# Six PSUM banks shared out two and four instead of three and three, in a two-layer encoder whose order a planner lays out

## The chip, the cores and the metric

The kernel runs on one core of a Trainium2 chip. The metric is the device time of one execution in microseconds (us), as the median of several runs. A profile of one execution shows when each engine worked: TensorE (PE, with its weight loads as PEld), VectorE (DVE), ScalarE (ACT), GpSimd (POOL), and SyncE (SP), which issues the DMAs.

## What is computed

The input is 512 positions by 1024 channels. Layer 0 is an RMSNorm, an input projection to 7168 channels, a gated convolution of width 3 (mixer A), a spatial gating unit with 128x128 position-mixing matrices (mixer B), an output projection and a residual. Layer 1 is another RMSNorm and projection, an RWKV-7 scan in both directions over 16 heads of 64 channels (mixer C), a 2-D Fourier transform over groups (mixer D), an output projection and a residual; a last RMSNorm follows. What matters here is layer 1, above all the scan:

```python
def wkv7_step(state, inp):
    r, w, k, v, a, b = inp
    sa = jnp.einsum('...ij,...j->...i', state, a)
    state = (state * w[..., None, :] + sa[..., :, None] * b[..., None, :]
             + v[..., :, None] * k[..., None, :])
    y = jnp.einsum('...ij,...j->...i', state, r)
    return state, y
...
def odd_layer(h, w_in, mu, w0, w2, a0, a2, k_k, k_a, r_k, lnx_g, lnx_b, fnet_w, w_out):
    p = jnp.einsum('bsd,de->bse', h, w_in)
    pc, zc, fd, zd = jnp.split(p, ODD_SPLITS, axis=-1)
    yc = rwkv7_bidir_branch(pc, mu, w0, w2, a0, a2, k_k, k_a, r_k, lnx_g, lnx_b) * jax.nn.silu(zc)
    yd = fourier_branch(fd, fnet_w) * jax.nn.silu(zd)
    return jnp.einsum('bse,ed->bsd', jnp.concatenate([yc, yd], axis=-1), w_out)
```

## The kernel before, in words

**Dense blocks.** Activations and weights are each split into a high and a low part, and a product is the sum of three (`mm3`, line 551). A dense block is one 128-channel slice of a projection for all 512 positions: 8 slices of the input times 3, so 24 products that add up in one PSUM bank (`pd_...`; `block0`, line 667, in layer 0, `block`, line 911, in layer 1). Layer 1 has blocks named `wa`, `k`, `r`, `v`, `zc`, `fd` and `zd`. DVE and ACT read a finished block out of PSUM (`evac`, line 946), and its bank is free then.

**The scan.** It is cut into chunks of 64 positions, and the heads into 8 units of two heads and two directions, numbered j = 0 to 7. A unit goes through these steps, and each turns on groups of small products whose results stand in PSUM until DVE and ACT have read them:

- `prep` (line 982): `zw` and `za`, decay and rate from a low-rank product; `half` (line 1059) then makes the operands `at`, `ops` on DVE.
- `sums` (`ss`), and `scores` (line 1095): `sm`, and for each half of the chunks `sa` and `sz`, which become `mt`, `am` and `zz`.
- `inverse` (line 1218): the inverse of a triangular matrix, first on DVE (`iL`, `iA`, `iT`, `iF`), then by the products `iH`, `iTT` and `iTB`, `iG`, `iTJ`; each needs what DVE or ACT made of the one ahead (`iTT` and `iTB` read `iHs`, which DVE makes of `iH`). The result is `dz`.
- `fold` (line 1301): `sp` of `zz` and `dz`, read out as `pt`; then `sg` of `ops`, `pt` and `am`, in four groups to a unit, read out as `gq` by a masked multiply on DVE and a copy on ACT.
- `chain` (line 1371): eight steps over the chunks, one after another. DVE makes `X` of `pa`, and PE makes the next `pa`, and the output `py`, of `X` and `gq`. Its tiles `pa` and `py` have a bank each.
- `bonus` (line 1194, `bo`) and `post` (line 1420, `vy`) finish the unit.

**The banks.** PSUM has eight banks here, in four rings. The ring `d` has three, for the dense blocks and for `zw`, `za` and `bo`. The ring `s` has three, for the other small products: `sm`, `sa`, `sz`, `sp` and `sg` take two each, one per head or direction, and ask for both at once (`both`, line 229); `iTT` and `iTB` take one each, at the same time. The output projections spread their four sums over the banks of several rings, by a tuple of tags (`project`, line 565; `project_o`, line 1542).

**The order.** The program is written as strands, generators that yield operations, and a planner (`Plan`, line 159) emits one operation at a time: it keeps a clock for each engine, and at each step takes the operation that can start first by these clocks, with some leaning to strands of lower rank. The chain has rank 0, scores, inverse and fold rank 1, dense blocks rank 5. A strand that asks a ring for a tile when none is free waits until another strand frees one. So the number of banks in a ring sets when a strand may go on, and with it the order on every engine. On the chip each engine then works its instructions off in that order, and waits by semaphores for operands and for banks.

Of the kernel before, what the change touches and what calls it, by code (L numbers as in the profile page):

```python
# [17 lines left out]
PSUM = bass.MemoryType.PSUM  # L18

P = 128  # L20
S = 512
D = 1024
KB = D // P
NS = S // P
C = 64
# [407 lines left out]
class K:  # L433
# [131 lines left out]
    def project(self, name, n, y, res, pair):  # L565

        for d in range(2):
            ps, tags = [None] * NS, (("d", "d", "d", "py"), ("s", "s", "s", "d"))[d]
            for bs in [(b,) for b in range(n - 3)] + ([(n - 3, n - 2, n - 1)] if d == 1 and pair else [(n - 3,), (n - 2,), (n - 1,)]):
                for b in bs:  # L570
                    yield f"w_{name}{d}_{b}"
                for s in range(NS):
                    if ps[s] is None:
                        ps[s] = yield from self.get(tags[s], f"p{name}{d}_{s}", [P, 512])
                    for b in bs:
                        w = self.w[f"{name}{d}_{b}"][0]
                        for e in range(2):
                            yield f"{y}{2 * b + e}"
                            l = self.out[y, 2 * b + e]
                            yield self.mm3(ps[s], self.part(l, slice(0, P), slice(s * P, (s + 1) * P)), self.part(w, slice(0, P), e),  # L580
                                           b == 0 and e == 0, b == n - 1 and e == 1)
                    if bs[-1] == n - 1:
                        self.plan.strand(2, res(d, s, ps[s], tags[s]))
                for b in bs:
                    self.used(f"{name}{d}_{b}")
# [956 lines left out]
    def project_o(self, d):  # L1542

        yield "bonus7"
        if d:
            for g in range(4):
                yield f"yo{8 + g}"
        else:
            self.gb = yield from self.get("vq", "fin_gb", [P, D])
            yield self.Q.dma_start(self.gb, self.I["fin_g"].to_broadcast([P, D]))  # L1550
        ps, tags = [None] * NS, (("d", "d", "d", "s"), ("pa", "s", "s", "py"))[d]
        def part(b, s):
            w = self.w[f"o{d}_{b}"][0]
            if ps[s] is None:
                if d == 1 and s in (1, 3):
                    yield ("y7_1", "vy7")[s // 2]
                ps[s] = yield from self.get(tags[s], f"po{d}_{s}", [P, 512])
            for e in range(2):
                yield f"yo{2 * b + e}"
                l = self.out["yo", 2 * b + e]  # L1560
                yield self.mm3(ps[s], self.part(l, slice(0, P), slice(s * P, (s + 1) * P)), self.part(w, slice(0, P), e), b == OUTS[0] and e == 0, b == OUTS[-1] and e == 1)


        last = OUTS[-LAST[d]:]
        for b in OUTS[:-LAST[d]]:
            yield f"w_o{d}_{b}"
            for s in range(NS):
                yield from part(b, s)
            self.used(f"o{d}_{b}")
        for b in last:  # L1570
            yield f"w_o{d}_{b}"
        if d:
            yield self.A.activation(self.fss[0][:, 2:3], self.eps["rms"], AF.Sqrt)
        for s in range(NS):
            for b in last:
                yield from part(b, s)
            self.plan.strand(2, self.res(d, s, ps[s], tags[s]))
        for b in last:
            self.used(f"o{d}_{b}")
# [57 lines left out]
    def run(self):  # L1637
        I = self.I
        with ExitStack() as ctx:
            self.cp = self.pool(ctx, "consts")  # L1640
            self.wp = self.pool(ctx, "weights")
            self.tp = tp = self.pool(ctx, "work")
            self.ip = self.pool(ctx, "scan")
            dram = self.pool(ctx, "dram", 1, bass.MemoryType.DRAM)
            dp, sp, yp, cp = (self.pool(ctx, name, n, PSUM) for name, n in (("dense", 3), ("short", 3), ("outs", 1), ("chain", 1)))
            self.h1 = dram.tile([S, D], F32, name="h1_dram")
            self.yd = dram.tile([6, P, S], F32, name="y_dram")
            fz = dram.tile([8, P, S], F32, name="f_dram")
            self.fz = {(kind, g): fz[4 * i + g] for i, kind in enumerate(("fd", "zd")) for g in range(4)}
            plan = self.plan = Plan(self.tc, self.nc)  # L1650
            self.T, self.V, self.A, self.G, self.Q = (plan.engine(e) for e in ("PE", "DVE", "ACT", "Pool", "SP"))
            self.h = tuple(self.cp.tile([P, KB, S], F32R, tag=n, name=n, bufs=1) for n in ("hh", "hl"))
            self.xw, self.units = [None, None], [(e, d) for e in range(2) for d in range(2)]
            self.rings = {}
            for tag, shape, bufs in (("lora", [P, 2, P], 2), ("xw", [P, 2, S], 2), ("k", [P, S], 2), ("r", [P, S], 2), ("w", [P, S], 2), ("a", [P, S], 2),
                                     ("kb", [P, S], 2), ("zg", [P, S], 3), ("bon", [P, S], 2), ("y", [P, S], 2), ("vq", [P, 2, S], 2),
                                     ("E", [P, 2, NCH, C + 1], 1), ("ops", [P, 4 * S], 4), ("at", [P, S], 2), ("q", [P, 1024], 5), ("pt", [P, 1024], 1), ("G", [P, 1024], 5), ("dz", [P, 16, C], 2)):
                self.ring(tag, shape, bufs)
            self.ring("lh", [P, 2, P], 1, dt=F32R)
            self.ring("hi", [P, 2, S], 1, dt=F32R)  # L1660
            for tag, shape in (("T", [P, 16, 16]), ("nr", [P, 2, 16]), ("F", [P, 16, 32]), ("A", [P, 16, 16]), ("A2", [P, 16, 16]), ("Dn", [P, 16, 32]), ("Dt", [P, 16, 32])):
                self.ring(tag, shape, 1, self.ip)
            self.ring("X", [P, 4, 64], 2, self.ip)
            self.ring("wq", [P, KB, P], 5, self.wp)
            self.ring("d", [P, S], 3, dp)
            self.ring("s", [P, 8, C], 3, sp)
            self.ring("py", [P, S], 1, yp)
            self.ring("pa", [P, 4, 64], 1, cp)
            self.blocks = [("wa", 0), ("k", 0)] + list(FIRST)
            self.gates = {}  # L1670
            for j in range(7):
                more = [(b, j + n) for b, n in ORDER if j + n < 8 and (b, j + n) not in self.blocks] + list(EXTRA.get(j, ()))
                self.blocks += more
                units = [(kind, q, k) for kind, q in more for k in range(KB)]
                for i, u in enumerate(units):
                    n = i * NCH // len(units) - SLACK
                    if n >= 0:
                        self.gates[u] = f"X{j}_{n}"
            V, G = self.V, self.G
            self.weights = [(f"pv{q}_{i}", I["w_ev"][q, i], [P, 4, 256]) for q in range(4) for i in range(2)]  # L1680
            at = {"xa": 0, "ba": 8, "ca": 16, "za": 24, "ub": 32, "zb": 48}
            for kinds in (("ub", "zb"), ("xa", "ca", "za", "ba")):
                self.weights += [(f"{b}{j}", I["w_e"][at[b] + j], [P, KB, P]) for m in range(4) for b in kinds for j in (2 * m, 2 * m + 1)]
            self.weights += [(f"e{d}_{b}", I["w_eo"][d, b], [P, 2, 512]) for d in range(2) for b in range(8)]
            at = {"wa": 24, "k": 8, "r": 0, "v": 16, "zc": 25, "fd": 33, "zd": 37}
            self.weights += [(f"{b}{j}", I["w_o"][at[b] + j], [P, KB, P]) for b, j in self.blocks]
            self.weights += [(f"o{d}_{b}", I["w_oo"][d, b], [P, 2, 512]) for d in range(2) for b in OUTS]
            self.w, self.wf, self.out, self.g = {}, {}, {}, [{"j": j} for j in range(8)]
            self.yh0, self.yl0, self.fss, self.h2 = {}, {}, {}, [None] * NS
            self.pool_r, self.pool_k, self.pool_t = FLAGS  # L1690
            for rank, gen in ((0, self.chain()), (1, self.start()), (1, self.build()), (3, self.post()), (4, self.loads()), (4, self.splits()), (4, self.prep()),
                              (5, self.products()), (6, self.params1()), (6, self.unit_states()), (FR, self.fnet()), (6, self.reload())):
                plan.strand(rank, gen, rank == 0, rank == 5)
            plan.run()
# [26 lines left out]
```

## Time and profile before

| what | value |
|---|---|
| runs | 1084.24, 1087.21, 1088.44 us; median 1087.21 |
| the profiled execution | 1090.07 us, of which its span is 1088.3 |
| PE busy | 1024.3 us, 94% of the span |
| DVE busy | 651.3 us, 60% |
| ACT busy | 472.7 us, 43% |
| POOL busy | 124.9 us, 11% |
| mean granted clock of TensorE | 0.983 |

The span is the time from the first to the last instruction of the profiled execution. A share of busy time is a mean over the whole span, and the stages differ: layer 0 takes the first 434 us, the eight units of layer 1 lie between 434 and 1036 us, and the last stretch is the output projection. An engine's idle time counts only where that engine sets the pace.

### The profile page before, as it was taken

The page shows a single profiled execution, that of the slowest core. Times are in us where ns is not written, and L with a number is a line of the kernel's source. Part 1 is how long each engine was busy: PE and PEld are TensorE (multiplying, and loading weights), DVE is VectorE, ACT ScalarE, POOL GpSimd, SP SyncE. Part 2 cuts the span into 40 slices and gives each one's busy share as a digit, 9 for nine tenths or more (in the row PEclk, how much of TensorE's full clock was granted, in tenths as well). Part 3 has the DMA queues.
Part 4 walks back from the last instruction along what each step waited for, and adds up shares of the span by engine and source line. Part 5 has one row for each costly group of instructions (what it writes and reads, how often), then busy time and mean ns, then how long its engine had stood idle before and what let it go on. Part 6 is the DMA issues. An engine that isn't in the chain of part 4 may idle for free. (4 is left out here: it accounts for less than half of the span.)

```text
span 1088.3 us, 27301 instructions
## 1 busy us (share of the span) xinstructions
PE 1024.3 (94%) x12024; PEld 839.3 (77%) x12024; DVE 651.3 (60%) x1225; ACT 472.7 (43%) x795; POOL 124.9 (11%) x155
## 2 busy tenths in 40 slices
PE   7999999999999999998898999989988899999997
PEld 6988888888888888876676778767767677777776
DVE  6464444344343336895795858867793976864453
ACT  7232222222222125753565455744644736453253
POOL 1001210010110010220012101321021201110000
PEclk9999999999999999999998999989998999999999
DMA  8322222322223332332012011110121111154033
GB/s 286 105 73 94 81 94 98 97 97 97 96 96 124 130 116 98 100 105 89 8 46 89 3 42 61 49 52 21 41 71 41 60 39 48 60 172 131 30 107 117
DMA packets 32663, 91.51 MB, mean 84 GB/s; under 512 B 4896, under 2 KB 7712, under 8 KB 32544
## 3 DMA queue, kind: packets, MB, share of 16 engines
q1 hardware_dynamic: 32544, 89.77, 25.1%
q8 instruction: 94, 1.54, 0.6%
q14 instruction: 25, 0.20, 0.1%
HBM read 81.82 MB, written 7.86 MB: 82 GB/s over the span
## 5 line engine op out<-in xcount | busy, mean ns | idle before, releaser
L401 PE MATMUL pe<-w_e,yh 128*128 128x512 f32 x256 | 81.5, 398 | 0.0
L401 PE MATMUL sg<-ops 64*128 64x128 f32 x512 | 66.6, 294 | 7.2 <-ACT am L401 2.1
L401 PEld LDWEIGHTS sg<-ops 64*128 64x128 f32 x512 | 53.9, 196 | 17.1 <-issue 3.9
L401 PE MATMUL sg<-pt,am 64*128 64x128 f32 x512 | 60.5, 283 | 0.0
L401 PEld LDWEIGHTS pe<-w_e,yh 128*128 128x128 f32 x256 | 48.1, 188 | 11.6
L401 ACT COPY gq<-sg 128x256 f32<-128x256 f32 x64 | 23.2, 370 | 71.7 <-DVE gq L401 70.5
L401 PEld LDWEIGHTS sg<-pt,am 64*128 64x128 f32 x512 | 52.3, 195 | 0.0
L401 PE MATMUL pd_zc<-hh,w_zc 128*128 128x512 f32 x128 | 50.5, 437 | 1.3 <-DVE w_zc L401 1.3
L401 PE MATMUL pe<-w_e,yl 128*128 128x512 f32 x128 | 50.3, 393 | 0.0
L401 DVE TENSOR_TENSOR w_e<-wf_e,w_e 128x1024 fp32r<-128x1024 f32 (+1 forms) x19 | 20.0, 1074 | 48.0 <-ACT w_e L401 47.8
L401 PE MATMUL pd_r<-hh,w_r 128*128 128x512 f32 x128 | 45.5, 409 | 2.0 <-DVE w_r L401 2.0
L401 DVE TENSOR_TENSOR gq<-sg,c_masks 128x256 f32<-128x256 f32 x64 | 25.6, 416 | 33.7 <-PE sg L401 33.7
L401 PE MATMUL pd_k<-hh,w_k 128*128 128x512 f32 (+1 forms) x144 | 44.6, 372 | 0.0
L401 PEld LDWEIGHTS pa<-X,gq 128*64 128x64 f32 x448 | 30.8, 139 | 17.1 <-issue 3.9
L401 ACT CAST w_e<-wf_e 128x1024 fp32r<-128x1024 f32 (+1 forms) x19 | 16.9, 913 | 62.4 <-PE pe L401 54.6
L401 PE MATMUL pd_v<-hh,w_v 128*128 128x512 f32 x128 | 43.8, 410 | 0.0
L401 PE MATMUL pa<-X,gq 128*64 128x64 f32 x448 | 38.8, 230 | 4.6 <-DVE X L401 2.0
L401 PE MATMUL pa<-c_cen,vq 128*64 128x128 f32 x256 | 42.6, 288 | 0.0
L401 PE MATMUL pd_ub<-hh,w_ub 128*128 128x512 f32 x128 | 40.5, 393 | 0.0
L401 PE MATMUL pd_zb<-hh,w_zb 128*128 128x512 f32 x128 | 40.4, 392 | 0.0
L401 PE MATMUL pd_xa<-hh,w_xa 128*128 128x512 f32 x128 | 40.4, 392 | 0.0
L401 PE MATMUL pd_ca<-hh,w_ca 128*128 128x512 f32 x128 | 40.4, 392 | 0.0
(362 smaller groups left out, 2831.4 us busy)
## 6 DMA issues: line engine op xcount, KB each, us to landing
wf_e<-in_w_eo SPq DMA_DIRECT2D x16, 512.0 KB
wf_o<-in_w_oo SPq DMA_DIRECT2D x12, 512.0 KB
wf_pv<-in_w_ev SPq DMA_DIRECT2D x8, 512.0 KB
wf_ub<-in_w_e SPq DMA_DIRECT2D x8, 512.0 KB
wf_zb<-in_w_e SPq DMA_DIRECT2D x8, 512.0 KB
wf_xa<-in_w_e SPq DMA_DIRECT2D x8, 512.0 KB
wf_ca<-in_w_e SPq DMA_DIRECT2D x8, 512.0 KB
wf_za<-in_w_e SPq DMA_DIRECT2D x8, 512.0 KB
```

Of the source, the lines that this page charges most:

```text
L401: i = op.call(*op.a, **op.kw)
```

## The change

Ring `d` gets two banks instead of three, and ring `s` four instead of three. Three tuples of tags follow: in each of the output projections one or two of the four sums move from a bank of `d` to one of `s`, or the other way. All planner constants stay, and every product is computed as before.

```diff
@@ project
-            ps, tags = [None] * NS, (("d", "d", "d", "py"), ("s", "s", "s", "d"))[d]
+            ps, tags = [None] * NS, (("d", "s", "s", "py"), ("s", "s", "d", "s"))[d]
...
@@ project_o
-        ps, tags = [None] * NS, (("d", "d", "d", "s"), ("pa", "s", "s", "py"))[d]
+        ps, tags = [None] * NS, (("d", "d", "s", "s"), ("pa", "s", "s", "py"))[d]
...
@@ run
-            dp, sp, yp, cp = (self.pool(ctx, name, n, PSUM) for name, n in (("dense", 3), ("short", 3), ("outs", 1), ("chain", 1)))
+            dp, sp, yp, cp = (self.pool(ctx, name, n, PSUM) for name, n in (("dense", 2), ("short", 4), ("outs", 1), ("chain", 1)))
...
-            self.ring("d", [P, S], 3, dp)
-            self.ring("s", [P, 8, C], 3, sp)
+            self.ring("d", [P, S], 2, dp)
+            self.ring("s", [P, 8, C], 4, sp)
```

Through layer 0 PE's order stays as it was; from the second dense block of layer 1 on it is laid out anew. It has the same 7720 matmuls. In an operation's name the first digit is the unit.

The first place is PE's order between the chains of units 0 and 1. Before, the group `sz1_1` (two banks), `ss2` (one bank) and `iTT1` with `iTB1` (two banks) stand close together:

```order
L401 MATMUL sz1_10_4939<-ops3_3213 64x128
L401 MATMUL sz1_11_4940<-ops2_3210 64x128
L401 MATMUL sz1_11_4940<-ops3_3213 64x128
L401 MATMUL ss2_4964<-sq2_4946,ones_98 32x256 x4
L401 MATMUL pd_v2_5041<-hh_84,w_v2_4970 128x512
L401 MATMUL pd_v2_5041<-hl_85,w_v2_4970 128x512
L401 MATMUL iTT1_5052<-iHs1_4795,iDt1_4764 32x32 x64
L401 MATMUL pd_v2_5041<-hh_84,w_v2_4971 128x512
```

And in the changed kernel, where `sz1_1` has moved into the chain of unit 0, and `ss2` behind `iTB1`:

```order
L401 MATMUL sz1_11_4788<-ops3_3213 64x128
L401 MATMUL py0_4508<-gq0_11_4676,X0_7_4764 64x64 x4
L401 MATMUL za2_0_4773<-xw0_3280,lh2_0_4368 128x512
L401 MATMUL iH1_4821<-iD1_4756,off_103 32x32 x64
L401 MATMUL pd_fd2_4987<-hh_84,w_fd2_4866 128x512
L401 MATMUL pd_v2_5007<-hh_84,w_v2_4908 128x512
L401 MATMUL iTT1_4984<-iHs1_4822,iDt1_4757 32x32 x64
L401 MATMUL iTB1_4985<-iDt1_4757,iHs1_4822 32x32 x32
L401 MATMUL ss2_5023<-sq2_5013,ones_98 32x256
```

Here one row stands for a dense block, and the blocks `k2` and `r2` are left out: between `sz1_1` and `iTT1` there are now most of `k2` and the whole of `r2`, `fd2` and `v2`, where two products of `v2` stood.

The second place is PE's order at the inverse of unit 5. Before, `iTT5` follows `iH5` at once:

```order
L401 MATMUL sa5_11_8509<-ops3_3213,at5_1_8017 64x128
L401 MATMUL iH5_8550<-iD5_8527,off_103 32x32 x64
L401 MATMUL iTT5_8676<-iHs5_8551,iDt5_8528 32x32 x64
L401 MATMUL pd_r6_8562<-hh_84,w_r6_8547 128x512
L401 MATMUL iTB5_8677<-iDt5_8528,iHs5_8551 32x32 x32
```

Now the dense block `r6`, and behind it `v6`, come between:

```order
L401 MATMUL za6_1_8718<-xw1_3325,ll_104 128x512
L401 MATMUL iH5_8632<-iD5_8567,off_103 32x32 x64
L401 MATMUL pd_r6_8797<-hh_84,w_r6_8682 128x512
L401 MATMUL pd_r6_8797<-hl_85,w_r6_8682 128x512
L401 MATMUL pd_r6_8797<-hh_84,w_r6_8683 128x512
```

The third place is the same step of unit 4. Before, dense products follow `iH4`:

```order
L401 MATMUL py3_7434<-gq3_01_7431,X3_3_7517 64x64 x4
L401 MATMUL iH4_7585<-iD4_7541,off_103 32x32 x64
L401 MATMUL pd_zc4_6963<-hh_84,w_zc4_6839 128x512
L401 MATMUL pd_zc4_6963<-hl_85,w_zc4_6839 128x512
L401 MATMUL pd_zc4_6963<-hh_84,w_zc4_6840 128x512
```

Now `iH4`, `iTT4` and `iTB4` stand in a row, and the dense block `r5` follows:

```order
L401 MATMUL za5_0_7711<-xw0_3280,ll_104 128x512
L401 MATMUL pd_k5_7093<-hh_84,w_k5_6856 128x512
L401 MATMUL iH4_7562<-iD4_7529,off_103 32x32 x64
L401 MATMUL iTT4_7801<-iHs4_7563,iDt4_7530 32x32 x64
L401 MATMUL iTB4_7802<-iDt4_7530,iHs4_7563 32x32 x32
L401 MATMUL pd_r5_7876<-hh_84,w_r5_7567 128x512
```

All through layer 1 the chains become more compact: the eight steps of a chain, with their `sp`, `sg`, `sz` and `sa`, now stand with few dense products between them in units 0 to 6, and the dense blocks stand together between the chains.

## Rows read from the trace of the kernel before

**Rows 1.** Busy time by stage: stretch; us, then PE, PEld, DVE, ACT, POOL busy, clock, DMA.

```profile
62.00:324.00 262.00, 262.00 (x1178) 216.22 (x1177) 117.20 (x142) 73.32 (x91) 27.78 (x16) 1.00 0.28 93
434.00:535.00 101.00, 91.94 (x1232) 72.31 (x1230) 76.07 (x134) 55.85 (x91) 14.44 (x23) 0.97 0.25 81
535.00:1036.00 501.00, 460.34 (x8478) 370.40 (x8478) 357.87 (x787) 259.18 (x477) 70.35 (x89) 0.97 0.18 58
```

**Rows 2.** The chain that ended last, at its end: start us, us, what.

```profile
1040.12 41.65 PE po L401 x180
```

**Rows 3.** Who PE waited for, 434 to 972 us: total us, times, longest.

```profile
PE iTT L401 <- DVE iHs L401: 7.5, 3, 3.3
...
PE iTT L401 <- DVE zz L401: 2.4, 1, 2.4
...
PE sm L401 <- ACT gq L401: 1.8, 2, 1.2
...
PE sg L401 <- ACT dz L401: 1.7, 2, 1.2
...
PE sg L401 <- ACT gq L401: 1.1, 2, 0.9
...
PE sz L401 <- ACT dz L401: 0.7, 1, 0.7
PE sa L401 <- ACT gq L401: 0.6, 1, 0.6
...
PE sg L401 <- ACT mt L401: 0.6, 1, 0.6
PE sm L401 <- ACT pt L401: 0.6, 1, 0.6
...
PE sa L401 <- ACT pt L401: 0.5, 1, 0.5
```

**Rows 4.** Timeline at 530 us: start us, us, instruction, count [idle before <-releaser].

```profile
530.21 0.30 PE L401 MATMUL sm<-at,ops 64*32 64x64 f32 x4
...
530.77 0.37 ACT L401 COPY gq<-sg 128x256 f32<-128x256 f32 x1 [2.51 <-DVE gq L401]
...
531.20 1.61 PE L401 MATMUL sm<-at,ops 64*32 64x64 f32 x124 [0.69 <-ACT gq L401]
```

**Rows 5.** Timeline of PE at 580 us.

```profile
580.25 1.93 PE L401 MATMUL iTT<-iHs,iDt 32*32 32x32 f32 x128 [2.38 <-DVE zz L401]
```

**Rows 6.** Busy time in the stretches behind that wait, as in rows 1.

```profile
580.00:590.00 10.00, 9.75 (x219) 7.98 (x221) 3.19 (x8) 4.39 (x8) 1.40 (x2) 0.67 0.29 94
590.00:600.00 10.00, 7.81 (x287) 5.92 (x273) 4.63 (x8) 5.47 (x12) 3.00 (x5) 0.83 0.24 71
```

**Rows 7.** Timeline in layer 0: a dense block read, the next but one begun.

```profile
80.38 0.60 ACT L401 ACTIVATE zb<-pd_zb 128x512 f32<-128x512 f32 x1
...
84.48 0.39 PE L401 MATMUL pd_ub<-hh,w_ub 128*128 128x512 f32 x1
```

**Rows 8.** Readers of ring d by tile: duration ns min/median/max, first and last start.

```profile
L401 DVE SCALAR_TENSOR_TENSOR rq<-pd_r,c_pv,rq x16: 740/744/751, 444.5 to 912.8; 128x511 f32<-128x511 f32 x16
L401 ACT ACTIVATE rq<-pd_r,omu x13: 667/686/692, 443.2 to 910.7; 128x512 f32<-128x512 f32 x13
L401 ACT ACTIVATE w<-zw,w0h x16: 667/687/714, 448.3 to 867.5; 128x512 f32<-128x512 f32 x16
```

**Rows 9.** Timeline of PE at the inverse of unit 5.

```profile
826.15 0.70 PE L401 MATMUL iTT<-iHs,iDt 32*32 32x32 f32 x58 [1.49 <-DVE iHs L401]
```

**Rows 10.** Timeline of PE in the chain of unit 0.

```profile
549.57 0.24 PE L401 MATMUL pa<-X,gq 128*64 128x64 f32 x1 [0.60 <-DVE iA L401]
```

**Rows 11.** Busy time in the chains of units 0, 2 and 4, as in rows 1.

```profile
535.00:561.10 26.10, 24.91 (x367) 20.70 (x368) 24.66 (x67) 11.98 (x25) 5.34 (x7) 1.00 0.09 27
...
665.30:684.50 19.20, 19.20 (x346) 16.58 (x346) 18.40 (x60) 7.64 (x18) 1.31 (x2) 1.00 0.14 47
...
800.40:846.60 46.20, 40.33 (x850) 32.97 (x850) 27.70 (x73) 20.32 (x42) 6.39 (x7) 0.93 0.11 34
```
## The prediction

> **What bounds the kernel now.** I read the busy time by stage first, since a share over the whole span says nothing of one stage. In layer 0 PE is busy for all of its 262 us, at full clock [rows 1]; there a change of banks can only cost. Between 434 and 1036 us PE is busy for 91.94 of 101 us and 460.34 of 501 us, so it stands idle for 9.1 + 40.7 = 49.8 us of 602, at a mean granted clock of 0.97 [rows 1]. DVE has 76.07 + 357.87 us of work there: it is not the bound on the whole, but it is near it in places. Last comes a stretch of output sums, 41.65 us of `po` at the end of the chain of waits [rows 2]. The question is therefore what of PE's 50 idle us hangs on banks. The waits of PE in 434 to 972 us name who released it [rows 3], and two timelines show how to tell a bank from an operand. In [rows 4] the first four products of `sm` go at 530.21, and the rest wait 0.69 us for the copy of `gq`, which ends at 530.77 + 0.37 = 531.14. `sm` does not read `gq`; what it needs is the bank that the copy empties. In [rows 5] `iTT` waits 2.38 us for DVE's `zz`, which it doesn't read either: `zz` empties the bank of `sz`.
>
> The profiled execution took 1090.07 us, 2.9 above the median of 1087.21. Terms are read in the former and taken off the median.
>
> **The change part by part.** PE has the same 7720 matmuls, with the same order through layer 0 and the same groups in the tail, so the change is one of waits.
>
> *Layer 0 and the tags of the output sums: 0.* A dense block is 24 products of about 262/1178 = 0.22 us, so some 5.3 us [rows 1]. With two banks a block must be read before the next but one begins. At the tightest of 56 places `pd_zb` is read until 80.38 + 0.60 = 80.98, and the next but one begins at 84.48: 3.5 us to spare [rows 7]. In the tail two of the four short banks hold output sums instead of one of three, which leaves two free, as before. Weights are loaded in the same sequence, and DMA is busy for a share of 0.18 [rows 1]; without that cover nothing changes either, as the bound there is PE.
>
> *A. Bank waits on the short ring: -10.0.* The entries of [rows 3] whose releaser writes a tile that the product does not read are 2.4, 1.8, 1.7, 1.1, 0.7, 0.6, 0.6, 0.6 and 0.5 us: 10.0. The fourth bank takes most of them away. As a second count I gave every group of the two orders the banks longest free, with reading done 1.1 us after the group for the first bank and 1.5 for the second, as `sg` and `gq` show: 40 reuses come too early before, by 20.3 us together, 5 after, by 1.6. That is an estimate, since an early reuse often hides behind another wait. The ends are 0 and -20; I take the measured waits. In the first place of the order, `ss2` and the pair of `sz1_1` no longer stand against `iTT1` at all.
>
> [...]
>
> *B. The clock behind the longest bank wait: -4.* [...] Now two whole dense blocks, `fd2` and `v2`, stand ahead of `iTT1`. The ends are 0 and -5; I take -4, since part of the second ten has other causes.
>
> *C. Two dense banks: +2.3.* Through the ring pass 89 tiles of layer 1: 41 blocks, 32 `zw` and `za`, 16 `bo`. A block `k`, `r` or `v` is read by two instructions of ACT and two of DVE, 2 x 0.686 + 2 x 0.744 = 2.86 us in a row; `zw` and `za` take 0.69 [rows 8]. Counting PE's work between a tile and the next but one in the new order, seven reuses come before the reading is over, by 2.3 us together (the longest 0.8 each, `fd1` behind `bo0`, `fd2` behind `za2`). Counted alike with three banks, the old order has three, of 0.4. PE works its instructions off in order, so behind such a wait stands everything that PE has next, the chain's `pa` or the inverse too, and whoever reads those; I count each in full. I take 2.3. The ends are 0, if DVE and ACT come early, and some +7.5, if each of the seven readers is about 0.75 us late (one more instruction in the queue ahead of it, 0.69 to 0.74 in [rows 8]).
>
> *D. The step from `iH` to `iTT`: +1.* Before, units 0, 3 and 5 wait here, 7.5 us in three waits [rows 3]; unit 5, where `iTT5` follows `iH5` at once, waits 1.49 in one piece [rows 9]. Unit 5 now has `r6` between, and unit 0 has dense work too, but `iTT4` stands right behind `iH4`, unit 7 has only `bo` between, and unit 3 stays. Three places remain for three, with a little less cover at one of them. Ends -5 (two of them gone, 2.5 each) and +5 (two more).
>
> *E. Chain steps with one small pair as cover: +2.* In a chain the next `pa` waits for DVE's `X`. Where nothing but one `bo` or `zw` stands between, PE waits 0.60 us [rows 10]. Before there was one such step, now there are five; four more by 0.6 is 2.4, of which I take 2. Ends 0 and +3.
>
> *F. More compact chains: 0.* The dense products inside the chains of units 0 to 6 were 24, 45, 9, 54, 60, 75, 18; now they are 0, 12, 21, 6, 0, 9, 6. They cover PE's waits for `X` and `gq`. The row nearest to the new state is the chain of unit 2, with nine: PE is busy for all of 19.20 us, DVE for 18.40 [rows 11]. So a chain carries itself, but DVE is full in it. I take 0; the ends are 0 and the second rival's +16.5.
>
> The sum: -10.0 - 4 + 2.3 + 1 + 2 = -8.7. From 1090.07 that gives 1081.4 for a profiled execution, and from the median **1078.5 us**.
>
> **The rivals.** *The waits return under another name (no change).* PE waits less for a bank and then as long for the operand that the same reader makes: `gq`, `pt` and `dz` are both the emptying of a bank and the input of the next step. For it speaks DVE with 24.66 of 26.1 us and 18.40 of 19.2 in two chains [rows 11]; against it that `sm` and `iTT` in [rows 4, 5] had all operands. With half of A and B back: -5 - 2 + 5.3 = -1.7, so 1085.5.
>
> *The compact chain becomes DVE-bound (slower).* Place: the chains of units 0 to 6. Without dense products between its steps PE waits for `X` and `gq` wherever DVE takes longer than PE. Price: the three chains of [rows 11] have 1.2, 0 and 5.9 us of PE idle, 2.35 in the mean; times seven that is 16.5, and 1078.5 + 16.5 gives 1095. It decides from the point where a chain takes more than about 2 us above its PE work (7 x 2 = 14, which with -8.7 makes +5.3). For it: DVE at 96% in unit 2. Against: there PE lost nothing, and unit 0, with 24 dense products, lost more than unit 2 with nine, so dense cover is not what sets it; unit 4's idle time holds the inverse too, which now stands outside.
>
> *The clock falls in the chains (much slower).* Small groups with pauses between could hold PE at the mixture of [rows 6]. Unit 2's 19.2 us less nine dense products of 0.22 is 17 us; at 0.67 it would be 25.4, 8.4 more, times seven 59: 1137. Against it: the clock is 1.00 in the chains of units 0 and 2, and 0.93 in unit 4 [rows 11]. [...]
>
> **How the numbers follow.** The forecast has 0.50, no change 0.27, the compact chains 0.20, the clock 0.03. The forecast does not stand higher because an order laid out anew moves waits that I have counted only in sum, and its gain is made of many terms of 2 us. The range goes from 1062, where the second count of A (-20.3) and all of B (-5) come and the costs are nil (1087.2 - 25.3), to 1098, the second rival with some 3 us more from C's upper end. About 0.5%, 5.4 us, is what a measurement of this kernel can tell from no change: below 1081.8 is faster, above 1092.6 slower. So faster 0.50, same 0.27, slower 0.23 (0.20 + 0.03).
>
> **What would show it.** In the new profile the waits of `iTT` for `zz`, of `sm` and `sa` for `gq` and of `sg` and `sz` for `dz` are gone or below 0.5 us (A), and the clock behind `iTT1` is near 1.00 (B). The first products of `fd1` and `fd2` wait a little for the readers of `bo` and `za`, and nothing else waits long for a dense bank (C). `iTT4` waits about 2.5 us for `iHs` (D). The chains of units 0 to 6 take 18 to 20 us each with PE hardly idle (F). PE's idle time from 434 us to the output sums falls from 50 to about 45 us, and less of the stretch is spent below full clock. I am wrong if that idle time stays or grows, whoever it is put down to: by waits for `X` and `gq` in the chains it is the second rival, by waits for `pt`, `dz` or `iHs` outside them the first, and by dense blocks waiting for their readers it is C at its upper end.

## The result, and the profile after

The changed kernel took 1094.19 us (median of 18 runs, 1088.65 to 1099.43) against 1088.19 us before (18 runs): ratio 1.0058, 95% interval 1.0039 to 1.0076. It is slower by 6 us, where 8.7 less was forecast. Here and below, ratios, clocks and losses leave out two single executions at a far lower clock, one of 1746 us at 0.712 (three and three banks, FETCH 4.2) and one of 1256 us at 0.749 (the old order written out). The profiled execution of the changed kernel took 1091.95 us, 1.9 more than that of before, and with 0.982 it has a higher mean clock than most of its runs. So the trace shows where the pauses went, and the runs what the clock took on top.

Busy time by stage of the changed kernel, the windows of [rows 1]:

```profile
62.00:324.00 262.00, 262.00 (x1178) 216.06 (x1177) 117.22 (x142) 73.50 (x91) 27.82 (x16) 1.00 0.29 93
434.00:535.00 101.00, 91.92 (x1215) 71.75 (x1215) 77.50 (x134) 56.99 (x93) 19.68 (x25) 0.97 0.25 81
535.00:1036.00 501.00, 458.50 (x8477) 369.08 (x8475) 361.94 (x790) 253.38 (x462) 84.22 (x93) 0.97 0.18 57
```

Layer 0 is as before, and so is the end of the chain of waits (compare [rows 2]):

```profile
1041.91 41.65 PE po L401 x180
```

Between 434 and 1036 us PE is idle for 9.1 + 42.5 = 51.6 us, where it was 49.8. That alone is no proof of more waiting: in the kernel before, profiled once more (`e1_before`), PE is busy for 91.83 + 462.37 us there, so idle for 47.8, and two executions of one kernel differ by 2.0. Who it waited for, 434 to 972 us, as in [rows 3]:

```profile
PE iTB L401 <- issue: 5.8, 2, 3.2
PE iTT L401 <- issue: 4.3, 4, 2.0
...
PE sg L401 <- ACT gq L401: 2.2, 4, 1.4
PE iTJ L401 <- DVE nt L401: 2.2, 1, 2.2
PE iTT L401 <- DVE iHs L401: 1.9, 2, 1.0
PE sa L401 <- issue: 1.9, 1, 1.9
...
PE pd_r L401 <- DVE kq L401: 1.8, 1, 1.8
PE za L401 <- DVE kq L401: 1.4, 1, 1.4
...
PE sm L401 <- issue: 1.4, 1, 1.4
```

Most of the bank waits of [rows 3] are gone: no `iTT` waits for `zz` and no `sm` for `gq`. In their place stand pauses named `issue`, in which nothing that the profile shows was missing (the trace of the kernel before has such pauses too, though [rows 3] leaves them out), and waits for a dense bank (`pd_r` and `za` for `kq`, which is made by reading `pd_k`). These are the longest of the kernel before, 434 to 972 us:

```profile
PE iTB L401 <- issue: 3.3, 2, 2.2
PE iH L401 <- issue: 3.3, 2, 2.1
```

I sorted all of PE's pauses of 0.25 us and more in the two timelines, 434 to 1037 us, by what ended them (places in PE's order are counted with its semaphore instructions):

| PE's pauses, us | before | after |
|---|---|---|
| a bank of the short ring | 9.8 | 3.9 |
| a bank of the dense ring | 0.9 | 6.7 |
| `iTT` for `iHs` | 7.5 | 1.9 |
| at the 193rd to 196th of each 256 PE instructions | 9.3 | 14.2 |
| a weight block not yet split | 3.4 | 2.0 |
| other operands of DVE, ACT, DMA | 16.7 | 21.1 |
| sum | 47.6 | 49.9 |

The second profile of the kernel before has 45.2 us in sum and 7.2 at that one place of 256, so a difference of 2 us in this table is within what single executions scatter.

The chains did become compact, and PE is hardly idle in them. Units 0, 2 and 4 of the changed kernel, to be read beside [rows 11]:

```profile
540.70:557.50 16.80, 16.18 (x338) 13.62 (x334) 15.91 (x55) 5.86 (x14) 1.89 (x2) 1.00 0.01 2
...
659.70:679.40 19.70, 19.30 (x420) 15.87 (x416) 14.41 (x37) 5.44 (x12) 1.51 (x3) 1.00 0.04 12
...
802.20:820.00 17.80, 16.32 (x339) 13.68 (x335) 16.87 (x56) 5.86 (x14) 2.14 (x3) 1.00 0.13 40
```

And the sums over the chains of units 0 to 6, first before, then after (time, then PE, PEld, DVE, ACT, POOL):

```profile
sum 217.20, PE 204.70 PEld 168.56 DVE 151.41 ACT 97.13 POOL 14.64; mean PE 29.24 PEld 24.08 DVE 21.63 ACT 13.88 POOL 2.09
```

```profile
sum 123.40, PE 120.03 PEld 100.47 DVE 107.99 ACT 44.60 POOL 7.91; mean PE 17.15 PEld 14.35 DVE 15.43 ACT 6.37 POOL 1.13
```

PE's idle time inside them fell from 12.5 to 3.4 us (the windows before are longer and hold more other work), and the clock is 1.00 in all seven after. What was gained there is lost between the chains, where the dense blocks, the inverse and the scores now stand. The inverse of unit 4 shows it (timeline of PE in the changed kernel):

```profile
758.87 1.29 PE L401 MATMUL iH<-iD,off 32*32 32x32 f32 x128
761.04 0.60 PE L401 MATMUL iTT<-iHs,iDt 32*32 32x32 f32 x46 [0.89 <-DVE iHs L401]
762.91 0.88 PE L401 MATMUL iTT<-iHs,iDt 32*32 32x32 f32 x81 [1.27 <-issue]
...
766.92 0.48 PE L401 MATMUL iTB<-iDt,iHs 32*32 32x32 f32 x18 [2.57 <-issue]
767.33 0.80 PE L401 MATMUL pd_r<-hh,w_r 128*128 128x512 f32 x1
```

`iTT4` waits for `iHs`, as forecast, but only 0.89 us. Then PE stops twice within a group whose operands are all there. Both stops are at the 194th of 256 instructions. Queue q8 explains them; this line is on the page of the changed kernel:

```profile
q8 instruction: 94, 1.54, 0.6%
```

PE has 24,048 instructions (12,024 products and as many weight loads), about 94 times 256, and q8 moves 94 packets of 16 KB. Each of the nine pauses of over 0.4 us at this place in the changed kernel, and each of the seven before, ends 1.2 to 1.6 us after such a packet landed, and no two packets start less than 3.2 us apart. The 128 products of `iH` above, 256 instructions with their loads, take 1.29 us. So PE waits for its code where small products use up 256 instructions faster than the next come: in the changed kernel each of its pauses at this place stands where the 256 instructions ahead had passed in 1.1 to 3.3 us. And behind these stops the clock falls (stretches around them, columns as in rows 1):

```profile
760.00:763.00 3.00, 0.84 (x73) 0.61 (x63) 3.00 (x5) 2.94 (x5) 2.92 (x2) 1.00 0.03 5
763.00:767.00 4.00, 1.43 (x133) 1.29 (x136) 1.37 (x2) 3.39 (x6) 2.02 (x3) 0.60 0.41 135
767.00:771.00 4.00, 4.00 (x27) 3.21 (x27) 1.02 (x2) 0.00 (x0) 0.00 (x0) 0.54 0.20 70
```

The dense products that follow run at 0.54, with PE busy throughout. In stretches of 0.5 us the clock reads 0.50 from 764.0 to 770.5 us and 1.00 from 771.0 on, and a dense product begins 0.43 us after the one ahead of it at 0.50, and 0.23 at 1.00.

The waits for a dense bank have a plainer cause. DVE reads `pd_k4` in two instructions with other work before and between them (timeline of DVE, then of PE, in the changed kernel):

```profile
690.20 0.75 DVE L401 SCALAR_TENSOR_TENSOR kq<-pd_k,c_pv,kq 128x511 f32<-128x511 f32 x1
...
691.78 1.17 DVE L401 TENSOR_TENSOR iT<-iT,iA 128x39 f32<-128x39 f32 x1
692.87 0.74 DVE L401 SCALAR_TENSOR_TENSOR kq<-pd_k,c_pv,kq 128x511 f32<-128x511 f32 x1
```

```profile
693.76 0.47 PE L401 MATMUL za<-xw,lh 128*128 128x512 f32 x1 [1.44 <-DVE kq L401]
```

So the bank stays taken for some 2.7 us after the first reading, and `za` begins only when the second one has ended, at 692.87 + 0.74 = 693.61.

### The profile page after: what moved, and what is told of

Same layout as the page of the kernel before. It is cut to its first block, busy times and chain, and to the rows that moved or that the text cites. A ratio compares the mean times of both kernels' runs of the same rounds, so it can differ in the third digit from the quotient of the medians.

```text
span 1090.1 us, 27340 instructions
## 1 busy us (share of the span) xinstructions
PE 1023.0 (94%) x12024; PEld 837.6 (77%) x12024; DVE 657.9 (60%) x1229; ACT 470.2 (43%) x785; POOL 144.0 (13%) x161
## 4 chain that ended last, share of the span: by engine, by line
PE 73%; DVE 16%; ACT 6%; issue 3%; DMA 1%; SPq 1%; DVEq 0%; ACTq 0%
PE pe L401 8%; PE po L401 6%; PE pv L401 4%; PE pd_zb L401 4%; PE pd_ub L401 4%; PE pd_xa L401 4%; PE pd_ba L401 4%; PE pd_za L401 4%; PE pd_ca L401 4%; PE pd_zc L401 3%; PE pd_r L401 3%; PE sg L401 3%; PE pd_v L401 3%; DVE iA L401 2%; PE pd_k L401 2%
## 5 line engine op out<-in xcount | busy, mean ns | idle before, releaser
L401 PE MATMUL sg<-ops 64*128 64x128 f32 x512 | 64.4, 288 | 5.7 <-ACT gq L401 2.2
L401 DVE TENSOR_TENSOR w_e<-wf_e,w_e 128x1024 fp32r<-128x1024 f32 (+1 forms) x19 | 20.0, 1074 | 48.1 <-ACT w_e L401 47.8
L401 PE MATMUL pd_ba<-hh,w_ba 128*128 128x512 f32 x128 | 40.4, 392 | 0.0
```

What stands on the lines that cost most here:

```text
L401: i = op.call(*op.a, **op.kw)
```

## The experiments

**The clock.** The clock of a run is its mean granted clock. One minus that, times the run's time, is at most what the time at the lower clock, 0.50 in the trace, costs; below this is called the clock loss, and the time less the loss the rest.

First the kernel before, unchanged.

> The kernel before, unchanged, for the granted clock of its single runs. The changed kernel had 0.974 to 0.982 in 18 runs, and its slow runs are those with a low clock (1097.7 at 0.974, 1086.8 at 0.982). Theory 1 (the changed order loses part of its time to the clock): the runs of the kernel before stand at 0.981 to 0.984, and 0.005 of 1090 us = 5 us of the difference between the medians is clock. Rival (the clock scatters alike in both): 0.974 to 0.983 here too, at the same times for the same clock.

1088.34 us, ratio 0.9994 [0.9968, 1.0021], clock 0.975 to 0.990. With the runs of the kernel before that came along in all comparisons there are 92: mean 1088.7 us, mean clock 0.9817, loss 20.0, rest 1068.7. The changed kernel's 18 runs: 1094.2, 0.9775, loss 24.6, rest 1069.6. Of the 5.5 us between the means 4.6 are loss and 0.9 the rest. Theory 1 holds in the mean, though single runs of the kernel before also go down to 0.973. The loss is an upper bound, and it tells that the clock was lower, not why.

**The order against the banks.** For three runs the planner was replaced by a table that holds the recorded order of every engine; rings and tags stay as they are in the code.

```diff
-            best, hold = None, self.held()
...
+            for e, q in queues.items():
+                if q and (best is None or q[0][0] < best[0]):
...
+                        op = op.other if q[0][2] else op
+                        if op.eng == e:
+                            best = q[0][0], s, op
```

Controls for it are the two kernels themselves, written out.

> The changed kernel's own order and banks, emitted from the written-out table that the second to fourth runs use: a control for them. Nothing differs but some semaphore waits at 16 of some 5700 rows of PE. Theory: 1092 to 1097, ratio 1.003 to 1.008, as the changed kernel itself. Rival (writing the order out costs by itself): 1098 or more, and the runs built on it stand against this one.

> The order and the banks of the kernel before, emitted from the written-out table: the control for the fourth run. Theory: 1086 to 1091, ratio 0.998 to 1.002, so that spreading the old order did cost 6 us. Rival (the writing out costs): 1092 to 1096, and spreading the old order changed nothing.

The new order: 1097.81 us, 1.0086 [1.0056, 1.0116], between the theory (to 1097) and the rival (from 1098), with an interval that overlaps that of the changed kernel. The old one: 1097.04 (median of nine runs), 1.0059 [1.0033, 1.0085]. There the rival holds: writing it out costs some 6 us by the ratio. The trace puts it in the last stretch, from the last `pa` to the end: 59.1 us against 52.8 in both kernels as they are, where the weights of the output projection come late (the chain that ended last in the written-out old order):

```profile
1057.80 1.06 ACT w_o L548
...
1058.88 1.24 DVE w_o L548
...
1060.14 5.47 DMA wf_o<-in_w_oo
```

In the new order the stretch takes 54.6 us, 2 more than 52.8. The runs on the table stand against their own control.

Next, the new order with the old banks (three and three, old tags; the same order on every engine, with the turns at the banks fitted to the old counts).

> The changed kernel's order on every engine, word for word, with three banks to each ring as before (only the tags of the output sums and the counts differ). It parts the order from the banks. Theory 1 (the banks do what the prediction said; the order around them costs): the waits for a dense bank go, which the changed kernel has for 6 us, and waits for a short bank come back, 10 to 20 us, so slower than the changed kernel by 5 to 13 us: 1099 to 1107. Rival (short banks matter little, since the same readers are waited for as operands): within 3 us of the changed kernel, or faster by the 6 us of the dense waits: 1088 to 1097.

1107.42 us, 1.0185 [1.0122, 1.0247], 10 us above its control. Against the control theory 1 holds. The bank waits are back (waits of PE, 434 to 990 us):

```profile
PE sa L536 <- ACT gq L536: 4.0, 3, 2.3
...
PE sz L536 <- ACT gq L536: 1.8, 2, 1.0
...
PE sm L536 <- ACT pt L536: 1.6, 3, 0.6
```

Sorted as in the table above, waits for a short bank take 12.1 us here and 4.8 in the control, those for a dense bank 1.4 and 6.4; the old order has 9.8 for its three short banks. So the new order leans on the fourth short bank. The traces don't show all of the 10 us: PE's pauses sum to 51.6 us against 50.1 in the control, and the last stretch takes 57.3 against 54.6. The two profiled executions even stand the other way round, 1102.28 us at 0.983 against 1105.90 at 0.969.

**The pauses for code.** In the new order dense products were moved into the long runs of small ones, in six places (two of them; numbers are places in PE's order).

> The changed kernel with 2 and 4 banks, and PE's order changed in six places alone: dense products that stand next to a long run of small products are moved into it (units 0, 1, 3, 4, 5, 7). The same products, the same order on every other engine. In these runs PE stands still for 14 us at places named issue, all at the 193rd to 196th of each 256 PE instructions, and 1.9 us for iHs. Theory 1 (those pauses are the loading of the next 256 instructions, and come where 256 pass in under some 4 us): they shrink to under 4 us in sum and the time falls by 8 to 12 us, 1082 to 1086, ratio to the kernel before 0.995 to 0.999. Rival (PE's pauses only show that DVE and ACT are the bound in these stretches): they come back as waits for operands, 1091 to 1096.

```diff
+MOVES = [
...
+    (5028, 5203, [(5028, 5092), (5188, 5196), (5092, 5124), (5196, 5199), (5124, 5156), (5199, 5203), (5156, 5188)]),
+    (5308, 5412, [(5308, 5324), (5332, 5348), (5348, 5380), (5324, 5332), (5380, 5412)]),
...
+]
```

1091.71 us, 1.0034 [1.0006, 1.0062], 6.1 below its control; the last stretch is alike in both, so the gain is in the units. The pauses at the 193rd to 196th instruction fell from 14.5 us in the control to 2.9, and the clock loss from 26.8 to 18.5; but the rest rose from 1071.2 to 1073.4, as PE now waits for operands and banks instead. Unit 4 again, in this run:

```profile
757.07 1.29 PE L555 MATMUL iH<-iD,off 32*32 32x32 f32 x128
760.66 0.47 PE L555 MATMUL pd_r<-hh,w_r 128*128 128x512 f32 x1 [2.30 <-DVE kq L555]
...
762.68 0.75 PE L555 MATMUL iTT<-iHs,iDt 32*32 32x32 f32 x64
...
766.70 0.47 PE L555 MATMUL iTB<-iDt,iHs 32*32 32x32 f32 x34 [0.17 <-issue]
```

Both theories hold in part: the code pauses of 1.27 and 2.57 us are down to 0.17, a wait of 2.30 for the dense bank of `k5` has come, and the clock stays at 1.00 here.

> The kernel before with its three and three banks, and PE's order changed in five places in the same manner (units 1, 3, 4, 5, 6). There the pauses at the 193rd to 196th instruction of 256 sum to 9 us, the wait of iTT for the bank that zz empties is 2.4, and those of iTT for iHs in units 3 and 5 are 4.8. Theory 1: the time falls by 8 to 14 us, 1075 to 1080, ratio 0.987 to 0.993; so the gain of spreading is as large without the fourth short bank. Rival: no change, 0.997 to 1.003.

The same for the old order, in five places: 1094.63 us, 1.0068 [1.0044, 1.0091], no different from its control (1.0059). Theory 1 fails, and against the control the rival holds: the pauses at this place only fell from 7.9 to 5.2 us, and the waits of `iTT` for `iHs` in units 0, 3 and 5 stayed or grew (3.9, 3.3 and 2.7 us). Unit 0 was not touched; in unit 5 dense products now stand between `iH` and `iTT`, but DVE makes `iHs` only 4.9 us after the end of `iH`. The wait of `iTT` for `zz` is gone. The clock loss did not fall with the code pauses: 23.0 us against 22.2 in the control.

**One bank by itself.** Two dense and three short banks, with the planner at work.

> Two dense banks and three short ones, laid out anew by the planner; the eighth bank serves one output sum of the last stretch alone. It prices the dense bank by itself. Theory 1 (the two halves of the change nearly cancel: the dense waits cost some 6 us, the fourth short bank gives back some 7): slower than the changed kernel by about 7, 1097 to 1104, ratio to the kernel before 1.008 to 1.014. Rival (the dense bank is hidden, and it is the fourth short bank that lets the planner lay small products close together and so makes the order slow): near the kernel before or faster, 1083 to 1091, ratio 0.995 to 1.003.

```diff
-            dp, sp, yp, cp = (self.pool(ctx, name, n, PSUM) for name, n in (("dense", 2), ("short", 4), ("outs", 1), ("chain", 1)))
+            dp, sp, zp, yp, cp = (self.pool(ctx, name, n, PSUM) for name, n in (("dense", 2), ("short", 3), ("tail", 1), ("outs", 1), ("chain", 1)))
```

1112.53 us, 1.0199 [1.0154, 1.0245]: slower than expected by 8 us, and the rival is out. Against the kernel before it lacks the third dense bank, which by the ratio is worth some 22 us; against the changed kernel it lacks the fourth short one, worth some 15 (1.0199 less 1.0058). The change takes the one and gives the other. Each of the two differences also holds what another order does by itself, up to 1.1% with a nudged constant and 2.8% with the halves below. So neither is the price of a bank; each is the price of a bank and one new order together.

**Other orders at either share of the banks.** A planner constant nudged, or the runs of small products cut in halves, gives another order with the same banks. Each was run at both shares; the first three are constants in `Plan`, the last is in `scores` and `inverse`.

```diff
-    BLOCK, FIRST, READ, FETCH = 256, 178, 33, 3.6
+    BLOCK, FIRST, READ, FETCH = 256, 178, 33, 4.2
...
-    SAFE, URGE, SWITCH, STAY, COLD = {}, 0.5, 0.2, 0.15, 2400.0
+    SAFE, URGE, SWITCH, STAY, COLD = {}, 0.5, 0.23, 0.15, 2400.0
...
-    LATE = {"": 0.2, "PE": 0.25, "ACT": 0.2, "DVE": 0.3, "Pool": 0.3, "SP": 2.5}
+    LATE = {"": 0.2, "PE": 0.25, "ACT": 0.22, "DVE": 0.32, "Pool": 0.3, "SP": 2.5}
...
-        yield self.plan.unit(*ops)
+        for n0 in (0, 32):
+            yield self.plan.unit(*ops[n0:n0 + 32])
```

> The changed kernel with one planner constant raised: the time that the planner reckons for loading the next 256 PE instructions, 3.6 to 4.2 us; the order is laid out anew. Theory 1 (the pauses at the 193rd to 196th of 256 instructions, 14 us in the changed kernel against 9 before, are worth avoiding by the planner itself): 1086 to 1091, ratio 0.998 to 1.003. Rival (they stand in for waits on DVE and ACT that come next anyway, as the spread order of the third run showed, whose pauses fell by 11 us and its time by 2.5; and any order laid out anew scatters by some us): 1090 to 1100, ratio 1.003 to 1.011.

> The kernel before, three and three banks, with the same constant raised from 3.6 to 4.2 us. Theory 1: 3 to 6 us faster than before, ratio 0.994 to 0.997. Rival (scatter of orders): anywhere within 8 us of the kernel before, ratio 0.993 to 1.008.

> The changed kernel with a constant nudged that has no cause to matter (the planner's cost of a change of tile shape, 0.20 to 0.23 us); the order is laid out anew with the same banks. Theory 1 (the 0.6% is the banks'): 1091 to 1097, ratio 1.003 to 1.009. Rival (the 0.6% is the luck of one order among many): outside that, by 4 us or more either way.

> The kernel before, three and three banks, with the nudge of the eighth run (0.20 to 0.23 us for a change of tile shape); order laid out anew. With two and four banks the orders so far stand at 1.006, 1.010 and 1.014 of the kernel before, with three and three at 1.000 and 1.005. Theory (the planner's constants fit the one order of the kernel before, and any other order loses, whatever the banks): 1.004 to 1.012, 1093 to 1102. Rival (three and three banks are better by themselves): 0.997 to 1.003.

> Two and four banks, the planner's cost of a change of tile shape 0.17 instead of 0.20 us. Theory: 1.005 to 1.014, clock loss 24 to 33 us, and above its partner, the next run. Rival (luck): below its partner as likely as above.

> Three and three banks, the same constant at 0.17. Theory: 1.000 to 1.010, clock loss 19 to 23 us, below its partner by 0.3 to 0.8%. Rival (luck): no order between the two.

> The changed kernel, two and four banks, with another nudge (what the planner adds for a hand-over from ACT 0.20 to 0.22 us and from DVE 0.30 to 0.32). Theory (scatter of orders about a middle of some 1.010): 1.003 to 1.016, 1092 to 1106, with a mean granted clock below 0.980 where the time is above 1095. Rival (this change of banks has a fixed price of 0.6%): 1.004 to 1.008.

> Three and three banks with the nudge of the twelfth run (hand-overs from ACT 0.22, from DVE 0.32 us); its partner with two and four stands at 1.0061. Theory (two and four banks cost some 0.5% by way of the clock, whatever the order): this one below its partner, 0.998 to 1.004, with some 20 us lost to the clock against 26. Rival (luck of the order): above its partner as likely as below.

> The changed kernel with the runs of small products cut in halves for the planner: the 64 of iH, of iTT and of sm are each two groups of 32, so that dense products can come between; order laid out anew with two and four banks. Theory (long runs of small products draw the pauses, and these the clock): clock loss down from 25 to about 20 us, ratio 1.000 to 1.004. Rival (the planner puts no dense products there, or pauses come back as waits on DVE and ACT): 1.005 to 1.012 at 24 us or more.

> The kernel before, three and three banks, with the 64 small products of iH, of iTT and of sm each cut in two groups of 32, order laid out anew: the partner of the sixteenth run, which stands at 1.0094. Theory (two and four banks cost some 0.4%, by the clock): below that, 1.001 to 1.008, with 3 to 8 us less lost to the clock than the 26 of its partner. Rival (luck of the order): 1.008 to 1.016.

| order | 3 and 3: ratio, clock loss | 2 and 4: ratio, clock loss |
|---|---|---|
| as it is | 0.9994 [0.9968, 1.0021], 20.0 | 1.0058 [1.0039, 1.0076], 24.6 |
| FETCH 4.2 | 1.0050 [1.0022, 1.0077], 20.3 | 1.0102 [1.0072, 1.0133], 30.6 |
| SWITCH 0.23 | 1.0109 [1.0068, 1.0150], 23.1 | 1.0143 [1.0107, 1.0179], 32.6 |
| SWITCH 0.17 | 1.0073 [1.0050, 1.0097], 27.9 | 1.0081 [1.0056, 1.0107], 27.4 |
| LATE 0.22, 0.32 | 1.0005 [0.9983, 1.0026], 16.7 | 1.0061 [1.0039, 1.0083], 25.6 |
| halves | 1.0279 [1.0237, 1.0321], 30.5 | 1.0094 [1.0065, 1.0123], 26.1 |

SWITCH 0.17 is the same line as above with 0.17 in place of 0.23. In five pairs three and three is ahead, by 0.1 to 0.6% (for the two SWITCH pairs that is within the intervals), and in four of these the clock loss is 4.6 to 10.3 us smaller; in the sixth it is behind by 1.9%. In this pair the code pauses are down to 4.4 us at three and three (9.4 at two and four), and waits for short banks and operands came instead (waits of PE, 434 to 990 us):

```profile
PE sg L401 <- ACT am L401: 7.3, 3, 3.9
PE iH L401 <- DVE iD L401: 4.9, 1, 4.9
...
PE sg L401 <- DVE zz L401: 4.2, 1, 4.2
```

A constant that has no cause to matter moves the time by up to 1.1% (SWITCH at three and three). The theory of luck is right about the size: the 0.6% lies inside what the order alone does. Raising FETCH, which makes the planner reckon with slower code, gained nothing at either share, as both rivals had it. SWITCH 0.23 came as luck would have it at two and four (1.0143, outside 1.003 to 1.009), and at three and three as the theory says by which any other order loses. LATE fits both expectations at two and four, and the theory at three and three. SWITCH 0.17 at three and three was expected at a loss of 19 to 23 us and has 27.9, so the theory of a price by way of the clock misses there. The halves missed twice: at two and four the code pauses fell from 14.2 to 9.4 us, but the loss stayed at 26.1 where some 20 was expected, and at three and three the time lies above both ranges.

One more reading of the table: the rest (time less loss) is smaller at two and four in four pairs, by 3.3 (FETCH), 4.7 (SWITCH 0.23), 2.1 (LATE) and 16.4 us (halves), and larger by 0.9 and 1.2 in the other two. That fits a fourth short bank that does what it was meant to, with a larger clock loss taking it back. No version beat the kernel before; the nearest is LATE at three and three, which can't be told from it.

What stays open is whether two and four banks would still lose on average over many orders. Five pairs of six say so, by 2.1% in sum, but the sixth alone is 1.9% the other way. The means over the six are 1.0085 and 1.0090. And no order found at three and three is faster than that of the kernel before, perhaps since its constants were chosen for it; without that first pair the means are 1.0103 and 1.0096. By these runs the share of the banks has no price that stands out from the orders.

## Why the prediction was wrong

*Wrong as a whole:* 8.7 us less were forecast, some 6 more came. That the time lies in the range, near the price of the second rival (1095), is luck: that rival's mechanism did not come.

*A, bank waits on the short ring, -10.0.* Right in kind, over-sized: the pauses fell from 9.8 to 3.9 us. One bank more does not leave the order as it was; the planner uses it to lay small groups closer together, and new waits come (`sg` for `gq`, 2.2 us).

*B, the clock behind the longest bank wait, -4.* This is the term that failed most. On the spot it came true in part. That wait is gone, and the stretches of [rows 6] now read:

```profile
580.00:590.00 10.00, 6.81 (x213) 5.25 (x212) 8.68 (x11) 5.00 (x8) 4.88 (x3) 0.99 0.17 57
590.00:600.00 10.00, 9.40 (x304) 6.20 (x303) 3.84 (x8) 4.15 (x9) 1.00 (x1) 0.84 0.23 70
```

That is 0.1 + 1.6 = 1.7 us below full clock instead of 5.0. The 5.0 are 3.3 us for the 0.67 of [rows 6] and 1.7 for the 0.83 of the second ten us. But they were never that wait's alone. The kernel before, profiled once more (`e1_before`), has the same wait, and the clock stays at 1.00 for 20 us behind it:

```profile
581.66 1.28 PE L401 MATMUL iTT<-iHs,iDt 32*32 32x32 f32 x128 [2.37 <-DVE zz L401]
```

```profile
581.40:591.40 10.00, 8.78 (x337) 7.20 (x337) 5.07 (x11) 6.34 (x13) 1.41 (x2) 1.00 0.30 96
591.40:601.40 10.00, 8.38 (x186) 6.03 (x186) 6.22 (x10) 4.99 (x10) 4.47 (x7) 1.00 0.23 70
```

And in the first profile the lower clock of the second ten us begins at a pause for code, not at the bank wait:

```profile
593.63 1.17 PE L401 MATMUL sm<-at,ops 64*32 64x64 f32 x65 [1.76 <-issue]
```

In the changed kernel PE is busy for only 6.81 us of the first ten, since `iTB1` waits 3.19 us for its code there, and the clock falls in other places, as behind `iTT4` above. Between 434 and 1037 us the two profiled executions lose 17.1 and 18.8 us to the clock, and the second profile of the kernel before 15.4. Over the runs the clock took 4.6 us more. So no run shows the -4: B is the term furthest off, by 8.6 us. The prediction took the clock's loss in one execution to belong to one wait. The traces show it at pauses of many kinds, and not at each of them. Of the seven falls before, three stand at pauses for code and four at waits for operands or a bank; of the nine after, five have a pause for code next to them and four do not. At 898.22 us of the changed kernel PE waits 1.76 us for a dense bank, and no fall follows.

With A and B at nothing the sum would have been +5.3; the runs show +5.5 to +6. That this sum is so near is luck: the +5.3 is C, D and E as I had priced them, and these came at +5.8, -5.6 and a small gain. Nor did A come to nothing; the bank waits that I read did go.

*C, two dense banks, +2.3.* Under-sized: +5.8. The two places named came as forecast (`fd1` and `fd2` wait 0.91 and 0.78 us), but the dense waits grew from 0.9 to 6.7 us. I took 2.86 us as the reading of a block in a row. In the trace its two DVE instructions wait their turn in a full queue: those for `pd_k4` begin 2.67 us apart, with `iT` and others between. The run with two dense and three short banks stands some 22 us above the kernel before, its new order included.

*D, from `iH` to `iTT`, +1.* It became -5.6: none of units 0, 3 and 5 waits for `iHs` any more. In unit 5 the dense blocks cover the step, and in unit 0 the group `sa` with its own pause for code. Unit 3 stayed as it was, with six products of `zc` between; there DVE makes `iHs` earlier, 0.8 us after the end of `iH` instead of 4.1. `iTT4` waits, as forecast, but 0.89 us.

*E, chain steps with small cover, +2, and F, compact chains, 0.* F was right: seven chains of 16.3 to 19.7 us with 3.4 us of PE idle in all. For E the trace shows a small gain: `pa` waits 2.2 us for `X` between 434 and 972 us, where it waited 3.3 for `X` and `iA`. The second rival is out by this, and the third too: the clock is 1.00 in the chains.

*The step that was missing.* "So the change is one of waits" (for banks and operands) put at nothing, without a reason, what PE's own instructions cost when they stand close. The kernel before already had 9.3 us of it, under the name `issue`. The dense products that left the chains now stand in blocks between them, and the inverse's small products next to each other. That costs PE 4.9 us more in waiting for code, and operands 4.4 us more, perhaps since less of DVE's work for the next unit lies beside a chain (that was not tried). The first rival comes nearest in kind, since waits came back under other names. But it named `gq`, `pt` and `dz` as operands, and most of what came back is code (4.9 us) and the dense banks (5.8). It was priced at half of A and B; in the trace all of the gain went, and the clock came on top.

What is shown and what is argued. That the pauses at one place of 256 are waits for code is shown by the packets. That they cost the new order time is borne out by the spread order: with 11.6 us less of them it took 6.1 us less than its control, and lost 8.3 us less to the clock. That they are what lowers the clock is not shown. SWITCH 0.17 and the halves at three and three have only 4.7 and 4.4 us of them and lose 27.9 and 30.5 us, more than the changed kernel. So which pauses make the 4.6 us of clock in this change stays open, and so does whether the banks have a part in the 6 us beyond the one order that the planner made of them.

## What to carry to other kernels

Where a planner lays out the order, a wait in the trace says what a resource costs in that order, not what one more is worth: 10 us of bank waits were read here, 5.9 went, and the time rose by 6 us, less than the order alone can make. A fall of the clock behind one wait in one execution says little of what that wait costs: profile the same kernel twice before you price it. Before a change of 0.5% is credited to a resource, lay out several orders at either setting; here a nudge without meaning moved the time by 1%, and over six orders the two shares of the banks came out alike. When a part becomes compact, look at what it used to cover, and read the stretches between the parts.

## What the hardware showed that I had not expected

PE's code comes in 94 packets of 16 KB, one for some 256 of its 24,048 instructions, and runs of small products can outrun it: ten pauses of 0.3 to 3.2 us in the changed kernel, each ending 1.2 to 1.6 us after a packet landed, 14.2 us in sum. The profile calls them "issue". Between dense products there are none: from 62 to 324 us, where 256 instructions take 26 to 29 us, PE is busy for all of the 262 us.

In the profiled execution of the kernel before, the granted clock fell seven times between 434 and 1037 us, each time at or shortly behind a pause of PE or several close together, and each fall cost 1.7 or 3.4 us (3.4 or 6.8 us at 0.50). Whether a fall comes varies from run to run: the wait of `iTT1` is 2.38 us in one execution and 2.37 in another, with a fall in the first and none in the second, and the kernel before itself ranges from 0.973 to 0.990. In the changed kernel the clock falls between the chains, as in the inverse of unit 4 (0.60 and 0.54 in the stretches behind `iTT4`), and not in the chains of units 0 to 6 (1.00 in all seven), where the third rival had looked.
